# GpSimd's elementwise work outside the mixers, done by VectorE

## The chip, the cores and the metric

The kernel runs on one core of a Trainium2 chip. The metric is the device time of one execution in microseconds (us). A core has five engines with a queue of instructions each: TensorE (PE; its weight loads are shown as PEld), VectorE (DVE), ScalarE (ACT), GpSimd (POOL) and SyncE (SP). Each works through its queue in order and waits on semaphores where an instruction needs what another engine makes. SP issues the loads here.

## The reference

Two layers of a diffusion backbone run over a latent stream x (512 tokens of 1024 features) and a context stream (256 tokens) with the same weights. Each layer has three sub-layers: a SwiGLU feed-forward network (FFN, half step), a mixer, and a second FFN. Before each sub-layer a stream is normed and modulated with shift and scale vectors, and its result is gated by a third; these adaLN vectors are products of SiLU(c) (or SiLU(c_ctx)) with `w_mod`:

```
silu_c, silu_cc = silu(c), silu(c_ctx)
mod_l = silu_c  @ w_mod[layer] + b_mod[layer]      # 3 sub-layers x (shift, scale, gate) x 1024
mod_c = silu_cc @ w_mod[layer] + b_mod[layer]
def macaron_ffn(x, g, shift, scale, gate, w_gu, w_down):
    h = rms_norm(x, g) * (1 + scale) + shift
    a, u = split(h @ w_gu, 2)                      # 2 x 2816 columns
    return x + 0.5 * gate * ((silu(a) * u) @ w_down)
```

The mixer of layer 0 is a neighbourhood attention beside a Fourier mixing, that of layer 1 a grouped-query attention beside a spatial gating unit. The output is the latent stream after layer 1; the last mixer and FFN need no context result.

## The kernel before, in words

All data are float32. Each operand of a large product is split in two float32r parts, high and low, and a product of two blocks is three matmuls (L303, L304, L305: high by high, high by low, low by high). ScalarE makes the high part (a cast, L324 in `fill`) and VectorE the low part (a subtraction of two tiles in SBUF, L325, written `wl`).

An FFN works through 22 tiles of 128 features of gate and up. A few of them are done directly (`lead`, `gu`), the others by Winograd's seven block products (`gu_w`): the weights come as four blocks a11, a21, a12, a22, each 128 x 512; four sums of blocks are made (L516, L517, L519, L522), and seven blocks are split by `put`. The input's blocks get the like sums once per FFN (`combos`: T1, T2, T3, -T4, lines 482 to 510). A gate and up tile is seven products of 12 matmuls, and VectorE and ScalarE turn their PSUM results into an activation and its split (L541 to L561, L414, L415). After every two to four tiles a chunk of the down projection follows: 8 blocks by one or two streams, each with a `residual` on VectorE (L316) that reads PSUM and x.

Between these, jobs make the adaLN vectors that later sub-layers need (`mod_jobs`, `mod_row`): a job loads 128 rows of `w_mod` (a half of 1024 columns, into one of two `wm` tiles) and multiplies them with silc along the row, once per stream, summing into one element per partition. For the latent stream VectorE does it in one instruction (L153, with a short read of the accumulator behind it). For the context stream GpSimd multiplies in place (L149) and ScalarE sums (L150). A `tick` after every product and every down block lets a job in when its share is due; FFN 0 of layer 0 has 96 jobs, FFN 1 of layer 0 has 80, both for two streams; FFN 0 of layer 1 has 64 for the latent stream alone.

The first FFN begins in `start_up`: for each of 8 k tiles two rows of `w_mod` (128 x 1024) are multiplied, norms are summed (`Norm.add`, L239), the weights of three tiles are split, and the products follow k by k; eight more rows come behind them.

GpSimd has, outside the mixers: L149 (200 instructions), the four sums of `gu_w` (74 each), five sums per k tile of `combos` (L486 to L488, L508, L509), the running sum of squares of all norms but the first two (L239), and one of three weight splits of `start_up` (L325). In the mixers it keeps splits of weights (L288), the bias negation and a product of the rotary embedding.

The order in which instructions stand in each engine's queue is set when the program is built, by a scheduler; the kernel ties some of it down with `issue_after`. In `mod_row`, L153 stands behind the last PSUM read of VectorE (`behind`), and L149 behind the last sum of `combos` (`pool_last`).

Of the kernel before, what the change touches and what calls it, by code (L numbers as in the profile page):

```python
# [20 lines left out]
P = 128  # L21
# [32 lines left out]
def hybrid_backbone_kernel(ctx: ExitStack, tc: tile.TileContext, A: dict, out: bass.AP):  # L54
# [9 lines left out]
    def opened(name, **kw):  # L64
        """a pool that is open from here until its second part is called"""
        es = ExitStack()
        return es.enter_context(tc.tile_pool(name=name, bufs=1, reuse_waits="tile", **kw)), es.close

    # PSUM: four banks, and four more that are single or in pairs as the phase wants them
# [20 lines left out]
    # ---------------------------------------------------------------- constants  # L90
# [13 lines left out]
    def load_constants(pool, l, shape):  # L104
        """per-head gains (those of the queries with the scores' factor, negated), head selectors and their transposes"""
# [14 lines left out]
    # ---------------------------------------------------------------- work that is emitted between groups of products  # L120
    pending = []
    down_last, act_last, pool_last = [], [], []
# [13 lines left out]
    # ---------------------------------------------------------------- adaLN vectors  # L136
    def load_silc(tiles, d0, n):
        """silu(c) and silu(c_ctx), n elements from d0, on every partition"""
# [5 lines left out]
    def mod_row(w, junk, silc, vecs, outs, behind=()):  # L144
        """products of 128 rows of weights with silc, an element of the vector per partition"""
        for v in vecs:
            if v == 1:
                with issue_after(pool_last):
                    POOL.tensor_tensor(w, w, silc[v], op=ALU.mult)  # L149
                ACT.activation(w, w, AF.Copy, accum_out=outs[v])  # L150
                continue
            with issue_after(behind):
                V.tensor_tensor_reduce(junk, w, silc[v], 1.0, 0.0, ALU.mult, ALU.add, outs[v])  # L153
# [16 lines left out]
    def mod_jobs(items):  # L170
        """items: (layer, sub, kind, vecs); a job takes 128 elements' products with a half of the features"""
# [23 lines left out]
    # ---------------------------------------------------------------- root mean square, inverse  # L195
# [4 lines left out]
    def rsqrt_sqrt(y, v, pool, shape, tag):  # L200
        """y = v ** -0.5; y and v: [p, n]: root, reciprocal and a Newton step"""
# [8 lines left out]
    def rsqrt_newton(y, v, pool, shape, tag):  # L210
        """the same, v normal and above 0, without the root: a first guess by exponent, then three Newton steps"""
# [7 lines left out]
    class Norm:  # L219
        """RMSNorm and modulation of columns [c0, c0+n) of x into hh, hl"""  # L220

        def __init__(self, c0, n, l, s, eng=POOL, room=None, tail=0):
            self.tail = tail
            self.c0, self.n, self.l, self.s, self.eng = c0, n, l, s, eng
# [3 lines left out]
        def add(self, kt):  # L228
# [4 lines left out]
            else:  # L233
# [5 lines left out]
                self.eng.tensor_tensor(self.acc[:, :self.n], self.acc[:, :self.n], sq[:, :self.n], op=ALU.add)  # L239

        def sums(self):
# [9 lines left out]
            (rsqrt_newton if self.eng is V else rsqrt_sqrt)(y[:, :nt], ms[:, :nt], sm, [P, nt], "rt")  # L251
# [29 lines left out]
    # ---------------------------------------------------------------- weight blocks, split in two float32r parts  # L281
    def wsplit(pool, r, bufs, tag="w", eng=V):
        """[128, n] -> two float32r parts, n at most 1024"""
# [7 lines left out]
    def wload(src, n=2048, parts=2):  # L291
        """one load of two blocks"""
# [4 lines left out]
    def by_k(w, k=KT):  # L297
        """split block [128, k * c] -> one (high, low) pair per k tile"""
# [8 lines left out]
    def issue_after(ins):  # L307
        """what is traced inside takes its turn on the engine behind ins"""
# [9 lines left out]
    # ---------------------------------------------------------------- half-step SwiGLU  # L318
    def fill(w, src, eng=V, behind=()):
        """a float32 block -> its two float32r parts"""  # L320
# [9 lines left out]
    def lead_ffn(fi):  # L330
        """the weights of the first three tiles, a part at a time; then where they are, and how to let go of them"""
# [1199 lines left out]
```

## Time and profile before

| | |
|---|---|
| time, median of 3 runs | 2843.02 us (2840.35 to 2845.91) |
| profiled execution, from first to last instruction | 2841.2 us |
| PE busy | 2648.6 us, 93%, 15826 matmuls |
| VectorE busy | 2188.0 us, 77% |
| ScalarE busy | 1213.8 us, 43% |
| GpSimd busy | 978.1 us, 34%, 677 instructions |
| granted TensorE clock, mean | 0.970 |

For the profiled execution only its span is given, 2841.2 us; the median of the runs is 1.8 us above it. A span from the first to the last instruction has stretches with different limits, so the views below are cut at the places where the work changes. Busy time of an engine counts from an instruction's start to its end; two instructions of VectorE can overlap by some hundredths of a microsecond, and busy time counts the overlap once. A mean duration of a group (line, operation, tiles, shape) holds what its instructions waited for after they had started. "Idle before" is the time in which the engine stood still ahead of a group, with what released it.

### The profile page before, as it was taken

What the parts mean: (1) busy time and instruction counts of PE and PEld (TensorE: products, weight loads), DVE (VectorE), ACT (ScalarE), POOL (GpSimd) and SP (SyncE); (2) the same over time, 40 slices, a digit from 0 to 9 for tenths busy, and PEclk for the clock granted to TensorE, in tenths of its full rate; (3) what the DMA queues carried; (4) which work ended last, traced back from release to release, by engine and by line L of the source; (5) the groups of instructions that cost most, each with busy time, mean ns of one, the idle gap of its engine ahead of it and who ended that gap; (6) DMA issues with size and microseconds to landing.
All of it is one profiled execution on the core that took longest, in us unless ns stands there. A gap on an engine that the chain in (4) does not pass through costs nothing.

```text
span 2841.2 us, 42081 instructions
## 1 busy us (share of the span) xinstructions
PE 2648.6 (93%) x15826; PEld 2393.1 (84%) x15826; DVE 2188.0 (77%) x3820; ACT 1213.8 (43%) x2512; POOL 978.1 (34%) x677
## 2 busy tenths in 40 slices
PE   3699999999999999899999988999999989999999
PEld 2589888987977788799899877999998767988988
DVE  8979889986466844998899877777777577577877
ACT  5334444444344542344444443333334455444443
POOL 4555545542121111555455323222212010143432
PEclk9899999999999999999999999999999999999999
DMA  6323333333111241133333321333323200303232
GB/s 236 106 75 117 123 110 123 112 114 117 63 55 48 67 158 38 49 123 113 121 112 108 99 83 53 107 104 108 115 97 104 81 31 1 119 35 108 93 108 90
DMA packets 81172, 271.69 MB, mean 96 GB/s; under 512 B 11002, under 2 KB 15518, under 8 KB 66248
## 3 DMA queue, kind: packets, MB, share of 16 engines
q1 hardware_dynamic: 80408, 268.76, 27.7%
q8 instruction: 124, 2.03, 0.3%
q14 instruction: 80, 0.66, 0.1%
q0 software_dynamic: 560, 0.24, 0.0%
HBM read 262.35 MB, written 5.24 MB: 94 GB/s over the span
## 4 chain that ended last, share of the span: by engine, by line
PE 62%; DVE 18%; ACT 4%; issue 3%; DMA 3%; POOL 2%; SPq 0%; DVEq 0%; ACTq 0%; POOLq 0%
PE ps L303 9%; PE ps L304 9%; PE ps L305 9%; PE pb L303 7%; PE pb L304 7%; PE pb L305 7%; DVE wl L325 5%; DVE junk L153 2%; PE pp L303 2%; PE pp L304 2%; PE pp L305 2%; PE ps L767 2%; ACT wh L324 2%; DVE xn L316 1%; DMA wm<-in_wmod 1%
## 5 line engine op out<-in xcount | busy, mean ns | idle before, releaser
L324 ACT CAST wh<-wr 128x512 fp32r<-128x512 f32 (+1 forms) x672 | 385.9, 590 | 571.6 <-PE pb L304 177.3
L325 DVE TENSOR_TENSOR wl<-wr,wh 128x512 fp32r<-128x512 f32 (+1 forms) x672 | 554.4, 837 | 93.7 <-ACT wh L324 88.8
L149 POOL TENSOR_TENSOR wm<-wm,silc 128x512 f32<-128x512 f32 x176 | 266.5, 1514 | 297.6 <-DVE mod L153 100.9
L303 PE MATMUL ps<-hh,wh 128*128 128x384 f32 (+2 forms) x728 | 252.1, 347 | 24.0 <-ACT u L541 18.9
L305 PE MATMUL ps<-hh,wl 128*128 128x384 f32 (+2 forms) x728 | 250.6, 344 | 2.2 <-DVE wl L325 1.2
L304 PE MATMUL ps<-hl,wh 128*128 128x384 f32 (+2 forms) x728 | 250.4, 344 | 0.0
L153 DVE CUSTOM_DVE_ANT_0 junk<-wm,silc 128x512 bf16<-128x512 f32 x240 | 225.2, 938 | 25.2 <-DMA wm<-in_wmod 20.1
L516 POOL TENSOR_TENSOR s<-wr 128x512 f32<-128x512 f32 x74 | 112.1, 1515 | 378.1 <-DMA wr<-in_wgs 245.8
L303 PE MATMUL pb<-hh,wh 128*128 128x384 f32 (+2 forms) x632 | 210.3, 333 | 29.6 <-ACT u L541 18.3
L304 PE MATMUL pb<-hl,wh 128*128 128x384 f32 (+2 forms) x632 | 209.4, 332 | 26.5 <-DVE hl L269 26.5
L303 PE MATMUL ps<-ah,wh 128*128 128x512 f32 (+1 forms) x640 | 218.9, 348 | 4.5 <-DVE u L560 3.7
L304 PE MATMUL ps<-al,wh 128*128 128x512 f32 (+1 forms) x640 | 220.7, 345 | 0.4 <-DVE al L415 0.4
L305 PE MATMUL ps<-ah,wl 128*128 128x512 f32 (+1 forms) x640 | 219.8, 344 | 0.0
L305 PE MATMUL pb<-hh,wl 128*128 128x384 f32 (+2 forms) x632 | 208.4, 330 | 0.2 <-DVE wl L325 0.2
L303 PE MATMUL pb<-tt,wh 128*128 128x384 f32 (+2 forms) x600 | 195.7, 326 | 13.5 <-ACT tt L481 13.5
L303 PE MATMUL pb<-ah,wh 128*128 128x512 f32 (+1 forms) x576 | 197.9, 354 | 7.6 <-DVE u L560 3.8
L304 PE MATMUL pb<-al,wh 128*128 128x512 f32 (+1 forms) x576 | 202.3, 351 | 2.5 <-DVE al L415 1.4
L304 PE MATMUL pb<-tt,wh 128*128 128x384 f32 (+2 forms) x600 | 196.4, 327 | 6.6 <-DVE tt L482 6.6
L305 PE MATMUL pb<-ah,wl 128*128 128x512 f32 (+1 forms) x576 | 200.8, 349 | 0.0
L305 PE MATMUL ps<-tt,wl 128*128 128x384 f32 (+1 forms) x600 | 195.6, 326 | 3.2 <-DVE wl L325 3.2
L303 PE MATMUL ps<-tt,wh 128*128 128x384 f32 (+1 forms) x600 | 195.3, 326 | 3.5 <-ACT wh L324 3.5
L305 PE MATMUL pb<-tt,wl 128*128 128x384 f32 (+2 forms) x600 | 195.8, 326 | 0.7 <-DVE wl L325 0.7
(373 smaller groups left out, 7379.1 us busy)
## 6 DMA issues: line engine op xcount, KB each, us to landing
wr<-in_wgs SPq DMA_DIRECT2D x76, 1024.0 KB
wm<-in_wmod SPq DMA_DIRECT2D x240, 256.0 KB
wr<-in_wdn SPq DMA_DIRECT2D x44, 768.0 KB
wr<-in_wdn SPq DMA_DIRECT2D x18, 512.0 KB
wr<-in_wgl SPq DMA_DIRECT2D x9, 1024.0 KB
wr<-in_wmod SPq DMA_DIRECT2D x16, 512.0 KB
wr<-in_wqk_ab SPq DMA_DIRECT2D x5, 1024.0 KB
bias<-in_bias_ab SPq DMA_DIRECT2D x12, 384.0 KB
```

Of the source, the lines that this page charges most:

```text
L149: POOL.tensor_tensor(w, w, silc[v], op=ALU.mult)
L153: V.tensor_tensor_reduce(junk, w, silc[v], 1.0, 0.0, ALU.mult, ALU.add, outs[v])
L303: PE.matmul(o, wh, rh, start=start, stop=False, skip_group_check=again)
L304: PE.matmul(o, wh, rl, start=False, stop=False, skip_group_check=again)
L305: return PE.matmul(o, wl, rh, start=False, stop=stop, skip_group_check=again)
L316: return V.scalar_tensor_tensor(xs, ps_ap, hgt[:, vec_index(c0), l * 3 + s, dt:dt + 1], xs, ALU.mult, ALU.add)
L324: ACT.copy(h[:, :n], src)
L325: eng.tensor_tensor(lo[:, :n], src, h[:, :n], op=ALU.subtract)
L516: POOL.tensor_tensor(f3, a11, a21, op=ALU.subtract)
L767: PE.transpose(out=o[:, c * P:(c + 1) * P], in_=p[:, c * P:(c + 1) * P], identity=ident)
```

## The change

All of GpSimd's work named above goes to VectorE; that of the mixers stays. The product for the context stream takes the form of the latent one, so that L149 and ScalarE's L150 become one more instruction of L153 each. The first two norms keep their way of a reciprocal root by a flag. The rest of the diff takes out comments. In the new file all lines behind `mod_row` stand five earlier (L153 is L148, L325 is L320, L547 is L542).

```diff
     pending = []
-    down_last, act_last, pool_last = [], [], []
+    down_last, act_last = [], []
...
         for v in vecs:
-            if v == 1:
-                with issue_after(pool_last):
-                    POOL.tensor_tensor(w, w, silc[v], op=ALU.mult)
-                ACT.activation(w, w, AF.Copy, accum_out=outs[v])
-                continue
             with issue_after(behind):
                 V.tensor_tensor_reduce(junk, w, silc[v], 1.0, 0.0, ALU.mult, ALU.add, outs[v])
...
-        def __init__(self, c0, n, l, s, eng=POOL, room=None, tail=0):
+        def __init__(self, c0, n, l, s, newton=False, room=None, tail=0):
...
-                self.eng.tensor_tensor(self.acc[:, :self.n], self.acc[:, :self.n], sq[:, :self.n], op=ALU.add)
+                V.tensor_tensor(self.acc[:, :self.n], self.acc[:, :self.n], sq[:, :self.n], op=ALU.add)
...
-            (rsqrt_newton if self.eng is V else rsqrt_sqrt)(y[:, :nt], ms[:, :nt], sm, [P, nt], "rt")
+            (rsqrt_newton if self.newton else rsqrt_sqrt)(y[:, :nt], ms[:, :nt], sm, [P, nt], "rt")
...
-                    sums(POOL, b, b22, b12)
+                    sums(V, b, b22, b12)
...
-                    POOL.tensor_tensor(a, b21[0], b, op=ALU.subtract)
-                    pool_last[:] = [POOL.tensor_tensor(a, a, b21[1], op=ALU.add)]
+                    V.tensor_tensor(a, b21[0], b, op=ALU.subtract)
+                    V.tensor_tensor(a, a, b21[1], op=ALU.add)
...
-                POOL.tensor_tensor(f3, a11, a21, op=ALU.subtract)
-                POOL.tensor_tensor(a21, a21, a22, op=ALU.add)
+                V.tensor_tensor(f3, a11, a21, op=ALU.subtract)
+                V.tensor_tensor(a21, a21, a22, op=ALU.add)
                 s1 = put(a21)
-                POOL.tensor_tensor(a11, a21, a11, op=ALU.subtract)
+                V.tensor_tensor(a11, a21, a11, op=ALU.subtract)
...
-                POOL.tensor_tensor(a12, a12, a11, op=ALU.subtract)
+                V.tensor_tensor(a12, a12, a11, op=ALU.subtract)
...
-                fill([a[:, (kt % 2) * 256:(kt % 2) * 256 + 256] for a in slots[i][kt // 2]], ws[i], POOL if i == 0 else V)
+                fill([a[:, (kt % 2) * 256:(kt % 2) * 256 + 256] for a in slots[i][kt // 2]], ws[i])
```

GpSimd's queue has 531 rows before and 35 now. In VectorE's queue the first place of interest is the beginning of `start_up`, from the first product of a `w_mod` row (L153; `ISA` with a `tt` or `wr` tile, and its read of the accumulator `mod 128x1`) on. Before:

```order
L153 ISA tt,mod<-wr,tt 128x1024
L153 ISA mod 128x1
L159 TENSOR_TENSOR mod<-mod,bmod 128x1
L239 TENSOR_TENSOR nacc<-nacc,t_172 128x512
L161 SCALAR_TENSOR_TENSOR gsc<-mod,ng 128x1
L153 ISA tt,mod<-wr,tt 128x1024
L153 ISA mod 128x1
L325 TENSOR_TENSOR wl<-tt,wh 128x256
L159 TENSOR_TENSOR mod<-mod,bmod 128x1
L325 TENSOR_TENSOR tt<-tt 128x256
L249 TENSOR_SCALAR ms<-ps 128x4
L213 TENSOR_SCALAR ry<-ms 128x4
```
Now:

```order
L148 ISA tt,mod<-wr,tt 128x1024
L148 ISA mod 128x1
L148 ISA tt,mod<-wr,tt 128x1024
L148 ISA mod 128x1
L154 TENSOR_TENSOR mod<-mod,bmod 128x1
L234 TENSOR_TENSOR nacc<-nacc,t_170 128x512
L148 ISA tt,mod<-wr,tt 128x1024
L148 ISA mod 128x1
L156 SCALAR_TENSOR_TENSOR gsc<-mod,ng 128x1
L320 TENSOR_TENSOR wl<-tt,wh 128x256 x2
L320 TENSOR_TENSOR tt<-tt 128x256
L148 ISA tt,mod<-wr,tt 128x1024
```
The first row's two products stand one behind the other now, and VectorE has all three weight splits of a k tile where it had two. Before, 4 products of rows stand ahead of `dg` (L253, from which the first norm's scale is spread to PE); now 15 do. Ahead of the low part of the last latent k tile of the normed input (`hl`, L269) there were 19, and there are 33.

The second place is a gate and up tile in the first FFN, beside the splits of a down projection's weights (`wl<-wr,wh 128x384`). VectorE before:

```order
L547 TENSOR_TENSOR u<-ps,u 128x384
L153 ISA junk,mod<-wm,silc 128x512
L153 ISA mod 128x1
L325 TENSOR_TENSOR wl<-wr,wh 128x384 x2
L551 TENSOR_TENSOR sg<-pb,u 128x384
L153 ISA junk,mod<-wm,silc 128x512
L153 ISA mod 128x1
L325 TENSOR_TENSOR wl<-wr,wh 128x384
L554 TENSOR_TENSOR u<-pb,u 128x384
L325 TENSOR_TENSOR wl<-wr,wh 128x384
L555 TENSOR_TENSOR u<-u 128x384
L556 TENSOR_TENSOR sg<-sg,u 128x384
```
Now:

```order
L148 ISA junk,mod<-wm,silc 128x512
L148 ISA mod 128x1
L320 TENSOR_TENSOR wl<-wr,wh 128x384
L546 TENSOR_TENSOR sg<-pb,u 128x384
L148 ISA junk,mod<-wm,silc 128x512
L148 ISA mod 128x1
L320 TENSOR_TENSOR wl<-wr,wh 128x384
L148 ISA junk,mod<-wm,silc 128x512
L148 ISA mod 128x1
L549 TENSOR_TENSOR u<-pb,u 128x384
L320 TENSOR_TENSOR wl<-wr,wh 128x384
L148 ISA junk,mod<-wm,silc 128x512
```
Between two PSUM reads (`u<-ps`, `sg<-pb`, `u<-pb`) there are now up to two products of a job row where there was one.

The third place is ScalarE's queue at such a tile, before:

```order
L150 ACTIVATE wm,mod<-wm 128x512
L324 CAST wh<-wr 128x512
L414 CAST ah<-sg 128x384
L541 COPY u<-pb 128x384
L324 CAST wh<-wr 128x512
L544 COPY u<-ps 128x384
L324 CAST wh<-wr 128x512 x2
L549 ACTIVATE sg<-pb 128x384
L150 ACTIVATE wm,mod<-wm 128x512
L324 CAST wh<-wr 128x512
L552 ACTIVATE sg<-sg 128x384
L150 ACTIVATE wm,mod<-wm 128x512
```
Now:

```order
L536 COPY u<-pb 128x384
L409 CAST ah<-sg 128x384
L319 CAST wh<-wr 128x512
L539 COPY u<-ps 128x384
L409 CAST ah<-sg 128x384
L544 ACTIVATE sg<-pb 128x384
L319 CAST wh<-wr 128x512 x3
L547 ACTIVATE sg<-sg 128x384
L536 COPY u<-ps 128x384
L319 CAST wh<-wr 128x512
L319 CAST wh<-s_2362 128x512
L319 CAST wh<-wr 128x512
```
The sums of job rows (L150), each of which reads what GpSimd's product leaves, are gone from between the casts of weights (L324) and the copies out of PSUM (L541, L544).

## Rows read from the trace of the kernel before

**Rows 1.** Part 1 of the page: busy us, share of the span, instructions.

```profile
PE 2648.6 (93%) x15826; PEld 2393.1 (84%) x15826; DVE 2188.0 (77%) x3820; ACT 1213.8 (43%) x2512; POOL 978.1 (34%) x677
```

**Rows 2.** Windows: busy us (instructions) per engine; PEclk, DMA share, GB/s last.

```profile
0.00:232.40 232.40, 160.79 (x798) 136.98 (x799) 199.40 (x299) 97.69 (x199) 124.45 (x78) 0.91 0.39 133
232.40:640.50 408.10, 383.44 (x2089) 362.50 (x2088) 365.50 (x594) 184.75 (x420) 214.90 (x145) 0.96 0.35 119
640.50:1200.00 559.50, 537.75 (x3453) 452.45 (x3452) 350.30 (x706) 236.32 (x458) 121.21 (x78) 0.98 0.22 75
1200.00:1635.00 435.00, 415.80 (x2321) 395.27 (x2320) 384.13 (x608) 193.64 (x432) 215.27 (x144) 0.98 0.33 112
1776.00:2184.70 408.70, 408.23 (x2324) 390.68 (x2323) 307.07 (x553) 147.32 (x278) 95.71 (x68) 1.00 0.32 107
2184.70:2842.00 657.30, 623.05 (x4194) 550.38 (x4193) 476.59 (x880) 299.47 (x621) 157.06 (x126) 0.98 0.21 74
```

**Rows 3.** Waits of the whole span: us in total, times, longest us.

```profile
ACT wm L150 <- POOL wm L149: 190.0, 136, 5.7
PE ps L303 <- ACT u L541: 18.9, 11, 3.1
PE pb L303 <- ACT u L541: 18.3, 9, 3.6
```

**Rows 4.** Timeline of VectorE, 290 to 295: start us, us, instruction.

```profile
290.45 0.68 DVE L325 TENSOR_TENSOR wl<-s,wh 128x512 fp32r<-128x512 f32 x1
291.05 0.55 DVE L415 TENSOR_TENSOR al<-sg,ah 128x384 fp32r<-128x384 f32 x1
291.52 1.78 DVE L325 TENSOR_TENSOR wl<-wr,wh 128x512 fp32r<-128x512 f32 x1
293.22 1.65 DVE L415 TENSOR_TENSOR al<-sg,ah 128x384 fp32r<-128x384 f32 x1
```

**Rows 5.** Timeline of GpSimd, the same stretch.

```profile
291.21 1.54 POOL L516 TENSOR_TENSOR s<-wr 128x512 f32<-128x512 f32 x1 [2.64 <-DVE wl L325]
292.82 1.63 POOL L517 TENSOR_TENSOR wr<-wr 128x512 f32<-128x512 f32 x1
```

**Rows 6.** Line 316: duration ns min/median/max, first and last start.

```profile
L316 DVE SCALAR_TENSOR_TENSOR xn<-ps,hgt,xn x184: 465/739/753, 1023.7 to 2837.2; 128x512 f32<-128x512 f32 x114, 128x256 f32<-128x256 f32 x70
```

**Rows 7.** Timeline of VectorE, 99 to 103.

```profile
99.80 0.15 DVE L161 SCALAR_TENSOR_TENSOR gsc<-mod,ng 128x4 f32<-128x4 f32 x1
99.87 2.83 DVE L269 SCALAR_TENSOR_TENSOR hl<-t,mod,hh 128x512 fp32r<-128x512 f32 x1
102.69 1.21 DVE L153 CUSTOM_DVE_ANT_0 tt<-wr,tt 128x1024 bf16<-128x1024 f32 x1
```

**Rows 8.** Groups by form, VectorE, 0 to 232.4: busy us, mean ns, idle before.

```profile
L325 DVE TENSOR_TENSOR wl<-wr,wh 128x512 fp32r<-128x512 f32 x27 | 25.0, 941 | 7.1 <-ACT wh L324 7.1
L424 DVE TENSOR_TENSOR al<-sg,ah 128x256 fp32r<-128x256 f32 x4 | 1.7, 423 | 1.4 <-ACT ah L423 1.4
L213 DVE TENSOR_SCALAR ry<-ms 128x2 int32<-128x2 int32 x1 | 0.7, 698 | 0.0
```

**Rows 9.** Groups by form, VectorE, 232.4 to 640.5.

```profile
L325 DVE TENSOR_TENSOR wl<-wr,wh 128x512 fp32r<-128x512 f32 x103 | 100.3, 980 | 8.7 <-ACT wh L324 7.6
L161 DVE SCALAR_TENSOR_TENSOR gsc<-mod,ng 128x8 f32<-128x8 f32 x4 | 1.7, 434 | 0.0
```

**Rows 10.** Groups by form, VectorE, 1200 to 1635.

```profile
L325 DVE TENSOR_TENSOR wl<-wr,wh 128x512 fp32r<-128x512 f32 x112 | 113.2, 1014 | 17.9 <-ACT wh L324 16.4
L163 DVE TENSOR_SCALAR hgt<-mod 128x8 f32<-128x8 f32 x2 | 1.4, 708 | 0.0
```

**Rows 11.** Groups by form, GpSimd, 232.4 to 640.5.

```profile
L149 POOL TENSOR_TENSOR wm<-wm,silc 128x512 f32<-128x512 f32 x85 | 127.5, 1499 | 143.9 <-DVE mpart L153 48.1 <-DVE mod L153 39.5 <-ACT wh L324 33.6
L522 POOL TENSOR_TENSOR wr<-wr 128x512 f32<-128x512 f32 x15 | 20.4, 1362 | 8.3 <-DVE wl L325 8.3
```

**Rows 12.** Groups by form, GpSimd, 1200 to 1635.

```profile
L149 POOL TENSOR_TENSOR wm<-wm,silc 128x512 f32<-128x512 f32 x76 | 115.8, 1523 | 134.0 <-DVE mpart L153 49.4 <-DVE mod L153 48.9 <-ACT wh L324 19.0
```

More of the change, by code (lines that the diff above doesn't have):

```diff
@@ L219, in hybrid_backbone_kernel @@
     class Norm:
-        def __init__(self, c0, n, l, s, eng=POOL, room=None, tail=0):
+        def __init__(self, c0, n, l, s, newton=False, room=None, tail=0):
             self.tail = tail
-            self.c0, self.n, self.l, self.s, self.eng = c0, n, l, s, eng
+            self.c0, self.n, self.l, self.s, self.newton = c0, n, l, s, newton
             self.room = room or (lambda: sm.tile([P, 512], F32, tag="t2", name="t2"))
@@ L660, in start_up @@
         nc.sync.dma_start(bmod, A["bmod"])
-        nl = Norm(*LAT, 0, 0, V)
-        nctx = Norm(*CT, 0, 0, V)
+        nl = Norm(*LAT, 0, 0, True)
+        nctx = Norm(*CT, 0, 0, True)
         def row(kind, kt, w):
```

## The prediction

> **What bounds the kernel now.** I read part 1 of the page first, then windows cut where the work changes, then the waits, then timelines of VectorE and GpSimd side by side, then groups by form. TensorE is busy for 93% of the span [rows 1], so the change can win or lose only where TensorE is not yet at its pace. That pace stands in the window of layer 1's first FFN, 1776 to 2184.7: 2324 matmuls, busy throughout, granted clock 1.00 (the 2.4 GHz level), 408.7 us [rows 2]. The like tiles of layer 0's second FFN, 1200 to 1635, have 2321 matmuls and take 435.0 us; so 26.3 us are lost there. Layer 0's first FFN, 232.4 to 640.5, has 2089 matmuls, at the same pace 2089 x 408.7 / 2324 = 367.4 us, and takes 408.1: 40.7 us are lost, at a mean clock of 0.96. The start, to 232.4, has TensorE busy for 160.8 us. In these three stretches VectorE is busy for 86 to 90% (199.4, 365.5 and 384.1 us) and GpSimd for about half (124.5, 214.9, 215.3), against 75% and 23% in the stretch that loses nothing.
>
> The timelines show what VectorE's busy time is made of. A weight split of 512 columns takes 0.68 us at 290.45 and 1.78 at 291.52; a split of 384 takes 0.55 at 291.05 and 1.65 at 293.22 [rows 4]. The long ones lie where GpSimd runs a sum, 291.21 to 292.75 and 292.82 to 294.45, and end just behind its end [rows 5]. They do not wait for data, for the engine is counted as running. A residual, which takes one operand from PSUM, never does this: 739 ns in the median, 753 at most, in 184 [rows 6]. So an instruction of VectorE that reads two tiles in SBUF stands still while GpSimd runs one, and GpSimd's work is paid for twice: on GpSimd, and in VectorE's queue.
>
> **What goes.** In each group of a window I take the count times what its mean lies above the duration of that form without GpSimd beside it: 0.68 us for 512 columns and 0.55 for 384 [rows 4], 0.42 for 256 [rows 8], 1.21 for a product of 1024 and 0.15 for a few columns [rows 7].
> - Start, 20 groups: from the weight splits, 27 x (0.941 - 0.684) = 6.9, to the last, 1 x (0.70 - 0.15) = 0.6 [rows 8]; sum 72.8 us.
> - First FFN, 11 groups: from 103 x (0.980 - 0.684) = 30.5 to 4 x (0.434 - 0.15) = 1.1 [rows 9]; sum 100.6.
> - Second FFN, 11 groups: from 112 x (1.014 - 0.684) = 37.0 to 2 x (0.708 - 0.15) = 1.1 [rows 10]; sum 103.6.
>
> **What comes.** Moved are 200 products, 296 sums of weight blocks, 80 of input blocks, 50 of squares and 8 splits. What one costs in a full queue is the step from its start to the next start: 0.60 for 512 columns (290.45 to 291.05) and 0.47 for 384 (291.05 to 291.52) [rows 4]. A product on VectorE already has the form it gets, so I take 0.61 for 512 and 1.14 for 1024 (1.21 less the same overlap); the read of its accumulator lies under the next instruction, at 0.
> - Start: 24 row products x 1.14, 11 of jobs x 0.61, 20 input sums x 0.47, 8 weight sums x 0.60, 8 splits x 0.34: 51.0 us.
> - First FFN: 85 products x 0.61 + 4 x 15 sums x 0.60 = 87.9 [rows 11].
> - Second FFN: 76 products x 0.61 [rows 12] + 4 x 17 sums x 0.60 = 87.2.
> The step is the low end, which no row undercuts. At the high end a sum costs its whole 0.68 and a product 0.08 more for the read of its accumulator, 0.76: 85 x 0.15 + 60 x 0.08 = 17.6 us more in the first FFN, some 17 in the second, some 8 in the start, 43 in all. I take the steps, since this queue is full.
>
> ScalarE loses L150, at 43% busy [rows 1]; by itself that is worth 0. But L150 waited 190.0 us in all for GpSimd, in a queue in which the copies of PSUM results stand behind it, and TensorE's waits for those copies (L541) are 37.2 us in both kinds of bank [rows 3]. I count them with the idle time below and not a second time.
>
> **The sum.** VectorE's load becomes 199.4 - 72.8 + 51.0 = 177.6 in the start (-21.8), 365.5 - 100.6 + 87.9 = 352.8 in the first FFN (-12.7), 384.1 - 103.6 + 87.2 = 367.7 in the second (-16.4). I let its idle time in each stretch stand (33.0, 42.6, 50.9 us): it waits for loads, casts and products as before, so a stretch gets shorter by what its load does. That is 210.6, 395.4 and 418.6 us, the last two above TensorE's 367.4 and 408.7, so that TensorE does not cut the gain off. In the start the scale of the first norm comes later, with 15 products ahead of `dg` where there were 4: 11 x 1.14 = 12.5 us, less the long instructions there; TensorE's first product comes some 6 us later. But the last latent k tile, whose split starts at 99.87 and takes 2.83 [rows 7], has 33 - 19 = 14 products more ahead of it, 16.0 us, against most of the 72.8 taken away; the start ends earlier.
>
> Elsewhere (640 to 1200, 1635 to 1776, and from 2184.7 on) I take 0. TensorE is busy for 96 and 95% of the two windows, VectorE for 63 and 73% [rows 2]: TensorE's products hide it. The last FFN gets 4 sums a tile; without cover these stretches could cost 10 us, and with the shorter instructions give 10. Layer 1's first FFN is at TensorE's pace and stays there.
>
> 2841.2 - 21.8 - 12.7 - 16.4 = 2790.3; the median stands 1.8 above the profiled span, so 2792. I take 2 off for waits behind L150: 2790.
>
> What speaks against it is the load of VectorE: 352.8 us against TensorE's 367.4 in the first FFN, 96%. The Trainium skill (Perfetto Trace Analysis, section Optimizing Scalar/DVE Operations) says that where VectorE is saturated, handing work to GpSimd can make sense, and it adds that the two share a read port of SBUF, so that it may not help. By the first half alone, undoing it would give the first rival's time; the steps of 1.78 against 0.68 us agree with the second half.
>
> **Rivals.**
> 1. Slower: the queue. All of it now hangs on one engine in order, with up to two job products between two PSUM reads, and TensorE waits for those reads to get its banks back. Price: idle time doubles in the three stretches, +126.5 us against -50.9: 2843 + 75.6 = 2919. It ends above before as soon as idle time grows by more than 50.9, some 40%. For it: 96%. Against it: VectorE was at 90% before and its stalls of 1.7 us were longer than any instruction it gets. 14%, with most of that near 2850.
> 2. Only the start gains; in the two FFNs idle time grows by what busy time loses, since TensorE's waits come from the order and not from the load: 2843 - 22 = 2821. For it: a load of 96% keeps a queue long. Against it: the second FFN's is 367.7 against 408.7, 90%. 14%.
> 3. All that is lost in the FFNs comes back, since GpSimd's legs of 1.3 to 1.6 us leave the chain from a load to a split: 2843 - 22 - 40.7 - 26.3 = 2754. For it: the stretch at 75% load loses nothing. Against it: no stretch here shows VectorE at 90% with TensorE never waiting. 14%.
> That the change does not do what it says can't be: GpSimd's queue has 35 rows left of 531.
>
> **How the numbers follow.** The forecast has 58%, for itself 2770 to 2833 (the 43 us of the dear end up, 10 us either way elsewhere, 10 of idle time down). The range reaches to both neighbours and leaves out the far end of the first rival: 2748 to 2842. A measurement of this kernel can tell 0.2%, 5.7 us, from no change. Faster: the forecast, rivals 2 and 3, less some of 2's upper end, 83%. Same 4%; slower 13%.
>
> **What would show it.** In the profile after: GpSimd busy for under 80 us; weight splits of 512 columns at 0.68 to 0.70 in the mean in both FFNs, and hardly a VectorE instruction over 1.3 us; VectorE busy for about 2140 us, hence nearly as long as before; the first FFN's tiles 10 to 15 us and the second's about 16 us shorter; the last latent split of the start before 90; TensorE's waits for L541 well under 37 us. It is wrong if the splits stay long without GpSimd, or if VectorE's idle time in the FFNs grows while its busy time falls; then TensorE's waits will name VectorE's reads of PSUM (L547, L551, L554, L560).

## The result and the profile after

The changed kernel takes 2744.89 us in the median (2742.79 to 2748.42, 4 runs), the kernel before 2844.28 (4 runs): ratio 0.9653 [0.964, 0.9667], 99 us less. The forecast was 2790 with a range of 2748 to 2842. The sign was right; the gain is nearly twice the forecast, and the time lies 3 us under the range.

The profiled execution has a span of 2741.0 us. Its busy times, which answer to [rows 1]:

```profile
PE 2613.9 (95%) x15826; PEld 2370.4 (86%) x15826; DVE 2168.1 (79%) x4654; ACT 1081.2 (39%) x2112; POOL 67.4 (2%) x43
```
VectorE runs 834 instructions more and is busy for 20 us less; I had said about 2140. Windows of the changed kernel, cut at the instructions at which [rows 2] is cut, to 0.3 us (us and count for PE, PEld, DVE, ACT, POOL, then clock, DMA share, GB/s):

```profile
0.00:193.80 193.80, 145.43 (x784) 125.70 (x785) 174.46 (x400) 65.21 (x129) 0.84 (x7) 0.98 0.46 158
193.80:565.90 372.10, 370.54 (x2109) 353.70 (x2109) 350.22 (x812) 131.22 (x250) 0.43 (x1) 1.00 0.40 130
565.90:1129.80 563.90, 537.22 (x3444) 451.65 (x3443) 363.83 (x798) 234.34 (x450) 56.30 (x26) 0.97 0.22 76
1129.80:1537.70 407.90, 407.90 (x2324) 390.65 (x2323) 361.30 (x810) 146.58 (x279) 0.00 (x0) 1.00 0.36 117
1679.40:2087.60 408.20, 408.20 (x2326) 391.09 (x2325) 316.75 (x621) 147.65 (x278) 0.00 (x0) 1.00 0.32 107
2087.60:2741.00 653.40, 623.27 (x4194) 551.63 (x4192) 493.49 (x996) 301.80 (x621) 9.86 (x10) 0.97 0.22 75
```
The start is 38.6 us shorter, the first FFN's tiles 36.0, the second's 27.1. In both FFNs TensorE is now busy but for 1.6 us, at a granted clock of 1.00 (where it was 0.96 and 0.98). VectorE's load there is 350.2 and 361.3 us, forecast 352.8 and 367.7. What I had not forecast is the idle time of VectorE: window less busy time, 33.0, 42.6 and 50.9 us before, is 19.3, 21.9 and 46.6 now. In the first FFN's tiles it is VectorE's waits for row tiles and for casts that went (us in total, times, longest), before:

```profile
DVE junk L153 <- DMA wm<-in_wmod: 13.7, 17, 1.4
DVE wl L325 <- ACT wh L324: 11.1, 13, 2.0
```
After, the casts' (that for row tiles is 0.3 us at most, the idle time of L148 below):

```profile
DVE wl L320 <- ACT wh L319: 4.2, 12, 0.6
```

Groups by form of VectorE in the first FFN's tiles, against [rows 9] (us, mean ns, idle before):

```profile
L148 DVE CUSTOM_DVE_ANT_0 junk<-wm,silc 128x512 bf16<-128x512 f32 x166 | 113.5, 683 | 0.3
L320 DVE TENSOR_TENSOR wl<-wr,wh 128x512 fp32r<-128x512 f32 x104 | 70.8, 685 | 3.4 <-ACT wh L319 3.1
```
The weight splits went from 980 ns to 685, those of the second FFN from 1014 [rows 10] to 685 as well. VectorE's timeline in the first FFN, as [rows 4] showed it before (start, us):

```profile
301.31 0.68 DVE L148 CUSTOM_DVE_ANT_0 junk<-wm,silc 128x512 bf16<-128x512 f32 x1
301.92 0.08 DVE L148 DVE_READ_ACCUMULATOR2_ANT mod<- 128x1 f32 x1
301.92 0.48 DVE L311 SCALAR_TENSOR_TENSOR x<-ps,hgt,x 128x256 f32<-128x256 f32 x1
302.32 0.68 DVE L320 TENSOR_TENSOR wl<-wr,wh 128x512 fp32r<-128x512 f32 x1
302.92 0.68 DVE L320 TENSOR_TENSOR wl<-s,wh 128x512 fp32r<-128x512 f32 x1
```
Steps of 0.60 to 0.61 us, and the accumulator's read lies under the next instruction: the prices of the sum hold.

TensorE's waits over the whole span, the two longest groups (total us, times, longest):

```profile
PE ps L242 <- DVE nacc L234: 24.9, 3, 18.2
PE ps L254 <- DVE dg L248: 23.5, 3, 19.2
```
Its waits for ScalarE's copies out of PSUM, 37.2 us in [rows 3], are gone from the list (the copy is L536 now). What leads it are norms, most of it in the start (18.2 and 19.2 us there, 16.4 and 14.9 before). ScalarE's waits in the first FFN's tiles show how far ahead the weights run. Before (232.4 to 640.5):

```profile
ACT wh L324 <- PE pb L304: 30.9, 18, 4.8
ACT wh L324 <- PE ps L304: 23.8, 19, 3.7
```
and after (193.8 to 565.9):

```profile
ACT wh L319 <- PE pb L299: 64.1, 37, 7.8
ACT wh L319 <- PE ps L299: 40.6, 34, 6.3
```
The cast waits for TensorE to give a weight tile back, 104.7 us in all instead of 54.7: the splits are ready earlier, and the feeding engines wait for TensorE more than it for them (1.6 us).

### The profile page after: what moved, and what is told of

It is laid out like the page before. It is cut to its first block, busy times and chain, and to the rows that moved or that the text cites. A ratio compares the mean times of both kernels' runs of the same rounds, so it can differ in the third digit from the quotient of the medians.

```text
span 2741.0 us, 41237 instructions
## 1 busy us (share of the span) xinstructions
PE 2613.9 (95%) x15826; PEld 2370.4 (86%) x15826; DVE 2168.1 (79%) x4654; ACT 1081.2 (39%) x2112; POOL 67.4 (2%) x43
## 4 chain that ended last, share of the span: by engine, by line
PE 85%; DVE 11%; DMA 1%; ACT 1%; issue 1%; SPq 0%; DVEq 0%; ACTq 0%
PE ps L298 12%; PE ps L299 12%; PE ps L300 12%; PE pb L299 11%; PE pb L298 11%; PE pb L300 11%; PE pp L298 2%; PE pp L299 2%; PE pp L300 2%; PE ps L762 2%; DVE xn L311 1%; PE ps L1073 1%; PE ps L1008 1%; DVE wl L320 1%; DVE junk L148 1%
## 5 line engine op out<-in xcount | busy, mean ns | idle before, releaser
L320 DVE TENSOR_TENSOR wl<-wr,wh 128x512 fp32r<-128x512 f32 (+1 forms) x672 | 431.2, 651 | 59.4 <-ACT wh L319 57.3
L148 DVE CUSTOM_DVE_ANT_0 junk<-wm,silc 128x512 bf16<-128x512 f32 x416 | 284.3, 683 | 3.2 <-DMA wm<-in_wmod 2.4
L300 PE MATMUL ps<-hh,wl 128*128 128x384 f32 (+2 forms) x728 | 245.1, 337 | 1.1 <-DVE wl L283 1.1
L298 PE MATMUL ps<-tt,wh 128*128 128x384 f32 (+1 forms) x600 | 194.5, 324 | 3.6 <-ACT wh L319 3.6
L299 PE MATMUL ps<-tt,wh 128*128 128x384 f32 (+1 forms) x600 | 194.5, 324 | 0.0
L311 DVE SCALAR_TENSOR_TENSOR xn<-ps,hgt,xn 128x512 f32<-128x512 f32 (+1 forms) x184 | 117.8, 644 | 40.4 <-PE ps L300 40.2
```

The costliest lines, as they stand in the source:

```text
L298: PE.matmul(o, wh, rh, start=start, stop=False, skip_group_check=again)
L299: PE.matmul(o, wh, rl, start=False, stop=False, skip_group_check=again)
L300: return PE.matmul(o, wl, rh, start=False, stop=stop, skip_group_check=again)
L311: return V.scalar_tensor_tensor(xs, ps_ap, hgt[:, vec_index(c0), l * 3 + s, dt:dt + 1], xs, ALU.mult, ALU.add)
L320: eng.tensor_tensor(lo[:, :n], src, h[:, :n], op=ALU.subtract)
```

## The experiments

All run beside the kernel before on the same chip. The table has the profiled span and, for the stretches of [rows 2], their length and, behind a stroke, VectorE's busy time; cuts at the same instructions. All but e9 and e10 ran once; e10 is the changed kernel again, and its stretches lie within 1 us of the first time. In the expectations L stands for the account in which VectorE's load and stalls set the length of a stretch.

| kernel | span | start | first FFN's tiles | to the second | second FFN's tiles | third to fourth |
|---|---|---|---|---|---|---|
| before | 2841.2 | 232.4 / 199.4 | 408.1 / 365.5 | 559.5 | 435.0 / 384.1 | 359.0 |
| after | 2741.0 | 193.8 / 174.5 | 372.1 / 350.2 | 563.9 | 407.9 / 361.3 | 365.6 |
| e1 jobs' products moved | 2788.0 | 225.9 | 379.7 / 360.2 | 563.8 | 408.2 / 366.7 | 361.7 |
| e2 weight sums moved | 2793.1 | 229.0 | 392.3 / 357.8 | 565.3 | 407.8 / 374.2 | 359.8 |
| e3 start-up moved | 2809.3 | 204.5 / 184.5 | 409.5 / 362.5 | 558.7 | 432.1 | 358.3 |
| e4 before, three row tiles | 2853.9 | 235.1 | 409.9 / 374.8 | 559.4 | 435.6 / 385.7 | 367.3 |
| e5 after + GpSimd reads | 2967.3 | 212.6 | 476.4 / 474.9 | 575.0 | 495.5 / 491.0 | 365.5 |
| e6 after + GpSimd writes | 2742.8 | 193.5 | 373.0 / 350.6 | 561.7 | 408.0 / 361.4 | 368.0 |
| e7 after + 2 splits' work a tile | 2762.6 | 194.3 | 375.7 / 358.4 | 580.7 | 409.7 / 379.7 | 364.7 |
| e8 after + 7 | 2853.1 | 203.1 | 414.9 / 409.8 | 584.7 | 448.2 / 433.0 | 364.5 |
| e9 norms' sums back | 2728.4 | 193.5 | 372.1 | 562.7 | 407.9 | 358.2 |
| e10 after, again | 2740.5 | 192.8 / 174.4 | 373.0 / 350.3 | 563.8 | 408.0 / 361.3 | 365.0 |
| e11 ScalarE sums again | 2754.5 | 203.8 / 175.6 | 380.7 / 351.2 | 560.4 | 407.4 / 360.0 | 364.3 |
| e12 input sums back | 2749.8 | 198.4 / 181.4 | 372.1 | 564.1 | 406.4 | 368.2 |
| e13 sums pass GpSimd | 2746.2 | 192.9 | 383.0 / 354.5 | 559.3 | 408.3 / 361.7 | 364.9 |
| e14 sums and jobs pass it | 2920.7 | 194.1 | 485.7 / 367.3 | 559.7 | 483.7 / 372.1 | 361.2 |
| e15 jobs pass it | 2746.9 | 193.6 | 373.1 / 347.2 | 576.2 | 405.7 / 360.7 | 364.4 |
| e16 e14 without ScalarE | 2885.5 | 193.8 | 466.4 / 366.8 | 559.0 | 462.6 / 370.8 | 364.7 |

### Parts of the change: e1, e2, e3, e4

e1 and e2 do one part each of the change, e3 the start's, and e4 gives the kernel before a third row tile, so that a job need not wait for ScalarE's sum:

```diff
# e1, in mod_row: only the start's rows keep GpSimd
-            if v == 1:
+            if v == 1 and behind is None:
# e2, in gu_w: all four sums
-                POOL.tensor_tensor(f3, a11, a21, op=ALU.subtract)
+                V.tensor_tensor(f3, a11, a21, op=ALU.subtract)
# e3: only the start's rows, and its weight splits
+            if v == 1 and behind is not None:
# e4
-NWM = 2
+NWM = 3
```


> The kernel before, with only the adaLN products of the jobs (176 of GpSimd's instructions and ScalarE's sums behind them) on VectorE; sums of blocks, norms and the start stay on GpSimd. Theory L (stalls): what the FFN bodies lost is VectorE standing still while GpSimd reads SBUF; the loss goes with GpSimd's busy time, of which the jobs are 127.5 of 214.9 us in the first FFN's body. Then the body (408 before, 372 changed) should come to about 384 to 389, the second FFN's (435 to 408) to about 416 to 420. Theory C (legs): the loss is waiting for GpSimd's and ScalarE's legs of a job, which hold the wm tile and ScalarE's queue; then nearly all comes back: 372 to 377 and 408 to 412. The start keeps its length in both: whole time about 2785 to 2800 by L, 2770 to 2780 by C.

> The kernel before, with only the four sums of weight blocks per tile (296) on VectorE. L: GpSimd loses 87 of 214.9 us in the first FFN's body, which should come to 392 to 398, the second's to 420 to 426. C: the jobs' legs stay, so the bodies stay within 5 us of 408 and 435. Whole time 2815 to 2830 by L, 2835 to 2850 by C (VectorE's load grows by some 80 us and nothing comes for it).

> The kernel before, with only the start's 24 row products and 8 weight splits on VectorE. The first Winograd tile's end (232.4 before, 193.8 changed) should come at 200 to 212 if these and not the jobs and sums behind them make the start's gain; the FFN bodies stay at 408 and 435 (within 4). Whole time 2812 to 2824.

> The kernel before with three wm tiles in place of two; no work is moved. C: in the first FFN's body VectorE stood idle for 13.7 us for loads into wm, which could be issued only when GpSimd and ScalarE had done with a tile; with a third tile the body falls by 10 to 16 us to about 395, the second's by 4 to 6. L: the stalls are as before, VectorE's idle time is only moved: both bodies stay within 4 us.

Times: 2789.83, 2794.85 and 2811.43 us against 2845.69, and e4 2855.79. Either half of the FFN work brings the second FFN to TensorE's pace by itself (408.2, 407.8), though GpSimd is still busy for 102.0 and 111.2 us there; so that gain doesn't add up from the two loads, as the sum had it. In e4 VectorE's waits for row tiles fall from 13.7 to 1.1 us in the first FFN, its busy time rises to 374.8, and no stretch gets shorter: these waits were not what held TensorE up. e3 gains 27.9 us in the start alone, of the 38.6. Against the expectations: e1's first FFN (379.7) lies between the two theories, its second is as C has it, its time as L has it; e2's first is as L has it, its second as neither has it, and its time is 20 us under L's; e3's and e4's stretches are as foreseen for L, e3's time 0.6 us under its range.

### GpSimd's reads against its writes: e5, e6

Both are the changed kernel with work on GpSimd behind every weight split of the first two FFNs, that nothing uses:

```diff
# e5
+    POOL.tensor_tensor(o[:, :n], w[0][:, :n].bitcast(F32), w[1][:, :n].bitcast(F32), op=ALU.mult)
# e6
+    POOL.tensor_scalar(o[:, :1], w[1][:, :1].bitcast(F32), -1.0, None, ALU.mult)
+    POOL.memset(o[:, :n], 0.0)
+    POOL.memset(o[:, :n], 0.0)
```


> The changed kernel, in which GpSimd multiplies the two finished halves of every weight block that put splits in the first two FFNs into a scratch tile that nobody reads (about 150 instructions of 1.3 us in each body, about as many as before the change). No engine waits for a result of GpSimd. Theory L (stalls): VectorE's splits and products are again stretched, 512 columns to 0.85 us or more in the mean, and with a load of 350 us and some 80 to 100 of stalls the first body comes to 430 to 470 us (372 changed), the second to 440 to 480 (408). Theory C (legs): no leg is in any chain, so both stay within 6 us of 372 and 408.

> The same, but GpSimd reads one column and then writes zeros twice over the scratch tile, so that it is busy for a like time and reads next to nothing. L, with the stall tied to GpSimd's reads: bodies within 6 us of 372 and 408, splits of 512 columns at 0.68 to 0.70. Rival: any work of GpSimd in SBUF stalls VectorE: as the kernel whose GpSimd reads, 430 and up.

2969.27 and 2744.57 us. Windows of the two FFNs' tiles, e5:

```profile
212.60:689.00 476.40, 400.01 (x2073) 373.55 (x2073) 474.85 (x812) 126.46 (x249) 220.84 (x154) 0.91 0.30 102
1264.10:1759.60 495.50, 437.44 (x2326) 408.68 (x2325) 490.96 (x810) 141.76 (x278) 244.55 (x169) 0.94 0.29 96
```
and e6:

```profile
193.50:566.50 373.00, 371.06 (x2111) 353.89 (x2110) 350.58 (x813) 131.32 (x250) 213.30 (x460) 1.00 0.39 130
1128.10:1536.10 408.00, 408.00 (x2324) 390.77 (x2323) 361.44 (x811) 146.62 (x279) 236.02 (x509) 1.00 0.35 118
```
GpSimd is busy for about as long in both. With two operands read, the same 812 instructions of VectorE take 124.6 us more; with fills and single columns, 0.4 more. So it is GpSimd's reads of whole tiles that stall VectorE, and not its writes; a read of one tile was not run. The Trainium skill (SBUF — State Buffer, section Who interferes with whom) says so: an instruction of VectorE with two inputs in SBUF contends with a GpSimd instruction that reads SBUF, and not with one that only writes. These two runs agree. e6 is as L has it; e5's tiles came out above L's ranges, by 6 and 16 us.

### VectorE's load alone: e7, e8

The changed kernel with products of 512 columns on VectorE, two or seven a tile in the first two FFNs, nothing on GpSimd:

```diff
+    V.tensor_tensor(o[:, :n], w[0][:, :n].bitcast(F32), w[1][:, :n].bitcast(F32), op=ALU.mult)
```


> The changed kernel with two more instructions of VectorE per Winograd tile of the first two FFNs (products of 512 columns into a scratch tile, 0.60 us each in a full queue): about 18 us more load in the first body (350 to 368 of 372), 20 in the second (361 to 381 of 408). My forecast's rule (VectorE's idle time stands, so a stretch changes by what its load does): bodies 390 and 428. Rival (TensorE's pace holds until VectorE's load passes it, idle time is what is left over): 372 to 378 and 408 to 410.

> The same with one more for each of a tile's seven blocks: about 63 us more load in the first body (413, over TensorE's 367), 71 in the second (432, over 409). Idle time stands: 435 and 479. TensorE's pace until the load passes it, then VectorE's: 413 to 424 and 432 to 442.

2764.37 and 2854.88 us. e7, the second FFN's tiles:

```profile
1150.70:1560.40 409.70, 408.18 (x2324) 390.85 (x2323) 379.70 (x847) 144.24 (x279) 0.00 (x0) 1.00 0.35 117
```
and e8:

```profile
1202.70:1650.90 448.20, 424.37 (x2334) 400.38 (x2333) 432.95 (x939) 143.03 (x277) 0.00 (x0) 0.97 0.31 106
```
18.4 us more load cost 1.8 us: VectorE's idle time gives way, from 46.6 to 30.0. In the first FFN VectorE's busy time rose by 8.1 of the 18 us, and the stretch by 3.6. A load above TensorE's pace shows in full, and then the stretch is the load and 5 us (first FFN) or 15 (second, 6 us above the range). This decides against "idle time stands", which wanted 428, and against the sum of the load as the reason for the 435.0 of before: 379.7 us without GpSimd take 409.7, 384.1 with it took 435.0. Most of what e7 loses it loses behind the first FFN (580.7), in one wait of TensorE for the norm's running sum, 16.5 us where the changed kernel waits 3.6.

### The norms' sums back: e9, e10

```diff
# e9, in Norm.add; e10 is the changed kernel itself
-                V.tensor_tensor(self.acc[:, :self.n], self.acc[:, :self.n], sq[:, :self.n], op=ALU.add)
+                self.eng.tensor_tensor(self.acc[:, :self.n], self.acc[:, :self.n], sq[:, :self.n], op=ALU.add)
```


> The changed kernel with one thing undone: the running sum of squares of the norms (all but the first two) is GpSimd's again. Theory L (behind an FFN TensorE waits for that sum in VectorE's queue, 3.6 and 3.1 us for the sum and 1.1 and 3.2 for dg, where it waited 0.2 and 0.5 before): the stretch from the first FFN to the second goes from 563.9 to 559 to 561 us, that from the third FFN to the fourth from 365.6 to 359 to 361, all else stands, time 2733 to 2739, 6 to 11 us under the changed kernel. Rival Q (the residuals that feed the sum are late, whoever sums): both stretches within 1.5 us of 563.9 and 365.6, time within 4 us of the changed kernel.

> The changed kernel itself, beside the last one on the same chip, so that the two can be told apart within some us. Both theories: 2742 to 2749.

Four runs of e9 and five of e10: e9 2734.39 us (2730.23 to 2736.01), ratio 0.9614 [0.9601, 0.9628]; e10 2742.23 (2740.82 to 2744.35), 0.9645 [0.9632, 0.9659]. The intervals do not overlap: e9 beats both kernels, by 8 us the changed one. TensorE's waits between the third FFN and the fourth, changed kernel:

```profile
PE ps L254 <- DVE dg L248: 3.2, 1, 3.2
PE ps L242 <- DVE nacc L234: 3.1, 1, 3.1
```
e9, same stretch:

```profile
PE ps L254 <- DVE dg L248: 3.0, 2, 2.2
```
The wait for the sum is gone but for 0.2 us, and the stretch is 7.4 us shorter, 0.8 more than foreseen. Between the first two FFNs it is only 1.2 of the 3 to 5 expected, for TensorE waits 4.0 us for the sum on GpSimd too; between the second and third it gains 3.5 (141.7 to 138.2), which I had not foreseen.

### ScalarE's sums and the input sums: e11, e12

```diff
# e11, in mod_row
+            if v == 1:
+                V.tensor_tensor(w, w, silc[v], op=ALU.mult)
+                ACT.activation(w, w, AF.Copy, accum_out=outs[v])
# e12, in combos: three sums and two of T3 and -T4 per k tile
-                    sums(V, b, b22, b12)
+                    sums(POOL, b, b22, b12)
```


> The changed kernel, but the context stream's products are made in place by VectorE and summed by ScalarE, so that ScalarE has its instruction back and GpSimd nothing. Theory L (the gain in the two FFNs comes from VectorE's load alone): the bodies of the two FFNs stay at 370 to 376 and 406 to 411 us, time 2740 to 2755. Theory S (ScalarE's sums in front of the copies out of PSUM, and the row tile that is held longer, had a share in what was lost): bodies 377 to 390 and 412 to 425 us, the waits of TensorE for L541 over 10 us in all, time 2755 to 2785.

> The changed kernel with the sums of input blocks (20 per FFN) back on GpSimd. Theory L: in the start, where VectorE is busy for 90%, GpSimd's sums make it stand still again, up to 20 x 1 us, part of it beside waits: start 196 to 206 us where the changed kernel has 193.8; in the stretches between FFNs within 3 us of 563.9, 141.7 and 365.6; time 2743 to 2758. Rival: VectorE's queue is what is short in the start, and 20 sums taken from it, 20 x 0.47, let the start end earlier: 184 to 190 us, time 2731 to 2740.

2756.27 and 2751.96 us. In e11 VectorE's load in the start is 175.6 (174.5 in the changed kernel) and ScalarE's 99.6 (65.2), and the start is 10.0 us longer; two of ScalarE's waits there:

```profile
ACT wr L150 <- DVE wr L149: 13.7, 10, 2.1
ACT tt L150 <- DVE tt L149: 6.2, 7, 2.4
```
So a part of the start's gain comes from ScalarE's queue. The first FFN gets 8.6 us longer, as theory S has it, the second not, as L has it, and the whole lies 1 us above L's range, in S's; but TensorE doesn't wait for L541, which was S's sign. It waits 3.8 us for VectorE's L415 and 2.4 for its L560, and three of its five pauses over 0.4 us go back to VectorE waiting for the load of a row tile (5.9 us of such waits in all): the row tile that is held longer, the other half of S. e12 is as L expected: 20 sums leave VectorE and its busy time in the start still rises by 7.0 us, the start by 4.6.

### GpSimd in the chain: e13 to e16

Open was what made the idle time. These are the changed kernel with tiles that pass through GpSimd after VectorE's work, nearly without reads: one column read, a fill of 512, one column times 1.0 in place. e13 does so with each sum of weight blocks, e15 with a job's row tile, on which ScalarE then sums; e14 has both; e16 is e14 without ScalarE.

```diff
+    POOL.tensor_scalar(o[:, :1], t[:, :1], 0.0, 1.0, ALU.mult, ALU.add)
+    POOL.memset(o, 1.0)
+    POOL.tensor_tensor(t[:, :1], t[:, :1], o[:, :1], op=ALU.mult)
+    ACT.activation(w, w, AF.Copy, accum_out=x)        # e14, e15: row tiles
```


> The changed kernel, and in the first two FFNs each of the four sums of weight blocks, made by VectorE, then passes through GpSimd: one column read, a fill of 512 columns, one column multiplied in place by 1.0, some 1.3 us, as long as GpSimd's sum took before, but with hardly a read. Theory W (VectorE's idle time before, 42.6 and 50.9 us, came from GpSimd's legs between a load and a split): bodies of 380 to 400 and 416 to 430 us. Theory B (legs are hidden by weights split ahead; what counts is VectorE's time at work, stalls included, where its load comes in bunches): 370 to 376 and 406 to 411 us. Both: splits of 512 columns at 0.68 to 0.75 us, start within 4 us of 193.8.

> The last kernel, and each row tile of a job of two streams, after VectorE's two products, passes through GpSimd in the same way and is then read by ScalarE in a sum that nothing uses: all legs of the kernel before on GpSimd and ScalarE in the two FFNs, without GpSimd's reads. Theory W: bodies of 395 to 410 and 425 to 437 us, as before the change (408.4 and 434.9). Theory B: 370 to 382 and 406 to 412 us; then what was lost before came from the reads of GpSimd alone.

> The changed kernel with the jobs' legs of e14 alone (GpSimd and ScalarE behind VectorE's two products, hardly a read by GpSimd), the sums' legs not. Theory G (what stands behind a job's leg in GpSimd's queue, the sums of weight blocks, is held back until VectorE comes to that job's products; either kind of leg alone costs little): bodies of 370 to 392 and 406 to 412 us. Theory S (ScalarE's sum stands in front of casts and waits for GpSimd): 430 us or more for both, as in e14 (485.7 and 483.7).

> e14 without ScalarE's sum: both kinds of legs through GpSimd, in its one queue, nothing of the jobs on ScalarE. Theory G: bodies of 440 us or more, GpSimd's column of a job waiting for VectorE's product up to 10 us with sums' columns behind it. Theory S: 370 to 392 and 406 to 415 us.

2748.45, 2922.48, 2748.64 and 2887.28 us. Either kind alone costs 4 to 6 us, little more than the changed kernel's runs differ (2740.8 to 2748.4), both together 180. e13's first FFN (383.0) is in W's range, its second (408.3) in B's; e14 is far over both; e15 is as G has it to 0.3 us. e14, first two FFNs' tiles:

```profile
194.10:679.80 485.70, 396.82 (x2118) 369.23 (x2117) 367.29 (x834) 189.68 (x427) 185.41 (x453) 0.92 0.30 100
1239.50:1723.20 483.70, 431.69 (x2322) 403.11 (x2321) 372.07 (x814) 194.02 (x428) 169.13 (x427) 0.95 0.29 98
```
VectorE does not stall here (its splits take 686 ns) and idles for 118.4 and 111.6 us. GpSimd's timeline in e14 says why (start, us; in brackets the idle time before and what ended it):

```profile
300.64 0.22 POOL L184 TENSOR_SCALAR scr<-wm 128x1 f32<-128x1 f32 x1 [1.14 <-DMA wm<-in_wmod]
300.92 0.53 POOL L185 MEMSET scr<- 128x512 f32 x1
311.77 0.48 POOL L186 TENSOR_TENSOR wm<-wm,scr 128x1 f32<-128x1 f32 x1 [10.33 <-DVE mod L148]
```
A job's instruction stands in GpSimd's queue for 10.33 us until VectorE comes to that job's product, and the weight sums behind it can't pass. ScalarE's casts then wait for the sums and TensorE for the casts; e16, first FFN, ScalarE:

```profile
ACT wh L324 <- POOL wr L405: 112.0, 42, 12.6
```
e16, whole span, TensorE:

```profile
PE ps L303 <- ACT wh L324: 74.0, 14, 16.8
PE pb L303 <- ACT wh L324: 39.0, 13, 10.0
```
So theory G holds for these kernels: ScalarE's part is some 20 us a stretch (e14 less e16), and only beside both kinds of tiles, and the shared queue makes the rest. GpSimd waits for VectorE's products in the kernel before too, in its first FFN's tiles:

```profile
POOL wm L149 <- DVE mpart L153: 48.1, 25, 7.6
POOL wm L149 <- DVE mod L153: 39.5, 22, 5.4
```
Whether that cost TensorE anything there, these lines don't say.

## Why the prediction was wrong

Right were the stall and its prices (980 to 685 ns, steps of 0.60), VectorE's loads (174.5, 350.2 and 361.3 us against 177.6, 352.8 and 367.7), that the last latent split of the start comes before 90 (77.9; e3 76.9), that the queue does not bind though it carries all (rival 1: VectorE is busy for 94% of the first FFN and TensorE waits 1.6 us), and that L541 goes.

**The step that failed** is "I let its idle time in each stretch stand (33.0, 42.6, 50.9 us): it waits for loads, casts and products as before, so a stretch gets shorter by what its load does". It gave 395.4 and 418.6 us for the two FFNs; they take 372.1 and 407.9, TensorE's own pace (it is busy for 370.5 and 407.9; the 367.4 of the forecast went by 2089 matmuls, of which the trace after has 2109). Of the 49.3 us between the sum, 2790.3, and 2741.0, 23.3 and 10.7 lie there and 16.8 in the start; the other stretches lost 1.5. The idle time was no property of VectorE's work: it is what is left over of TensorE's pace, and e7 shows it give way to load.

Why did TensorE pause before, at 384.1 us of load, and not in e7, at 379.7? Its waits in the first FFN's tiles, before:

```profile
PE ps L303 <- ACT u L541: 10.9, 5, 3.1
PE pb L303 <- ACT u L541: 9.1, 4, 3.6
PE ps L303 <- DVE u L560: 3.7, 1, 3.7
```
In the second FFN's they are of the same kinds, 15.3 us for L541 and 3.8 for L560. None is for a weight. Of the 20 pauses over 0.4 us in the two stretches, 15 go back, in ScalarE's queue, to a cast of an activation (L414) that waited for VectorE's L556 or L561, and two to VectorE's L560. In the 8 us before each of these 17, VectorE's instructions took 2.5 to 4.3 us longer than the shortest of their forms. One pause of 3.57 us, in the timelines of VectorE, GpSimd, ScalarE and TensorE:

```profile
379.25 1.60 DVE L153 CUSTOM_DVE_ANT_0 junk<-wm,silc 128x512 bf16<-128x512 f32 x1
381.25 1.77 DVE L153 CUSTOM_DVE_ANT_0 junk<-wm,silc 128x512 bf16<-128x512 f32 x1
383.57 1.61 DVE L556 TENSOR_TENSOR sg<-sg,u 128x384 f32<-128x384 f32 x1
379.01 1.29 POOL L522 TENSOR_TENSOR wr<-wr 128x512 f32<-128x512 f32 x1 [2.14 <-DVE wl L325]
380.94 1.54 POOL L149 TENSOR_TENSOR wm<-wm,silc 128x512 f32<-128x512 f32 x1 [0.64 <-DVE mod L153]
383.12 1.65 POOL L149 TENSOR_TENSOR wm<-wm,silc 128x512 f32<-128x512 f32 x1 [0.63 <-DVE mod L153]
385.21 0.51 ACT L414 CAST ah<-sg 128x384 fp32r<-128x384 f32 x1 [1.97 <-DVE sg L556]
386.15 0.63 ACT L150 ACTIVATE wm<-wm 128x512 f32<-128x512 f32 x1
386.78 0.46 ACT L541 COPY u<-pb 128x384 f32<-128x384 f32 x1
387.28 0.69 PE L303 MATMUL pb<-hh,wh 128*128 128x384 f32 x1 [3.57 <-ACT u L541]
```
Three instructions of VectorE take about 1 us longer than without GpSimd, each beside one of GpSimd's. The cast waits for the third; a job's sum (L150, between cast and copy in 12 of the 15) and the copy follow it, and TensorE waits for the copy. So a stall costs more than its share of VectorE's load, which is how the sum counted it: it delays the results that TensorE needs out of PSUM. e5, in which GpSimd's results feed nobody, has the same waits: 33.5 of TensorE's 76.4 us of pauses in the first FFN's tiles are for L541.

What came out is rival 3's time for the FFNs, nearly all that was lost there, to which I gave 14%. I held against it that no stretch showed VectorE at 90% with TensorE never waiting; what no trace shows yet is not evidence against it. But its reason, "GpSimd's legs of 1.3 to 1.6 us leave the chain from a load to a split", is not what these pauses show. e14 and e16 make 92 to 118 us of idle time out of GpSimd's place in the chain, but there TensorE waits for casts of weights, which it never did in these stretches before; and e13 and e15 keep one kind of leg, without reads, and lose 10.9 and 1.0 us in the first FFN and none in the second.

Shown are that idle time gives way (e7, e8), that GpSimd's reads stall VectorE (e5, e6), and that the pauses before stood behind such stalls. Not shown is how the gain divides between the stalls and L150's place in ScalarE's queue: no run takes the stalls away and leaves all else of the kernel before.

**The start** was to be 210.6 us and is 193.8. Its load was right within 3; its idle time fell from 33.0 to 19.3. VectorE's waits for ScalarE shrank: before [rows 8] it idled 7.1 us ahead of weight splits and this much ahead of the input's low parts:

```profile
L482 DVE TENSOR_TENSOR tt<-tsum,tt 128x384 fp32r<-128x384 f32 x16 | 12.0, 771 | 7.0 <-ACT tt L481 7.0
```
After, start:

```profile
L320 DVE TENSOR_TENSOR wl<-wr,wh 128x512 fp32r<-128x512 f32 x26 | 17.7, 689 | 2.6 <-ACT wh L319 2.4
L477 DVE TENSOR_TENSOR tt<-tsum,tt 128x384 fp32r<-128x384 f32 x16 | 8.7, 554 | 1.3 <-ACT tt L476 1.3
```
10.2 of 13.7 us. I had put ScalarE's lost instruction at 0; e11 prices it at 10.0 in the start. TensorE's first product comes 4.2 us later (some 6 foreseen), but its waits for the low parts of the normed input (L269), 26.5 us in the start before, are 3.0 after.

**Elsewhere** I took 0 within 10 us either way. It is +4.4 between the first two FFNs and +6.6 between the last two, where the norm's running sum now stands in VectorE's queue (e9 takes back 1.2 and 7.4), and -10.4 in the last FFN, whose weight sums leave GpSimd (282.8 to 272.4; e2 alone 273.7, e1 281.9).

## What to carry to other kernels

Before keeping an engine's idle time constant in a sum, ask what it waits for and whether the change takes that away: a stretch is as long as the slowest engine's work once nobody's queue holds up another's, and here a feeding engine at 94% did not show. Where one engine stalls another, don't count the stalls as load alone: look at what stands behind the stretched instructions and who waits for it. Look in a helper engine's queue for an instruction that waits for the engine it helps, with urgent work behind it; with two kinds of work in one queue the price is not the sum of the two (e13 to e16). And move a chain's last link (here the norm's running sum) only where the new queue is short: that link alone, put back, gave 8 us.

## What was not expected of the hardware

GpSimd's fills cost VectorE nothing: 213.3 us of fills and single columns beside its work in the first FFN added 0.4 us to it, while 220.8 us of products of two tiles (e5) added 124.6. And TensorE's pauses cost more than their length: in the first FFN its busy time fell from 383.4 to 370.5 us for the same products when its pauses went from 24.7 to 1.6 us, with the granted clock from a mean of 0.96 to 1.00, the 2.4 GHz level throughout; in e14, with 88.9 us of pauses, it is 396.8 at 0.92.
